# Squares of W_qkv taken during the output visits of layer 0, and a weight's low half ahead of the gate on VectorE

## The chip, the cores and the metric

The kernel runs on one core of one Trainium2 chip. The metric is device time in microseconds (us), smaller is better; a time is the median of several executions. The engines are TensorE (PE, matmuls), VectorE (DVE), ScalarE (ACT), GpSimd (POOL) and SyncE (SP), which issues the transfers (DMAs).

## The reference, cut to what matters

A trunk of two layers on x of 1024 rows and 1024 columns, in float32. Layer 0 mixes rows by a gated linear recurrence (RG-LRU), layer 1 by stick-breaking attention. Each mixer is followed by a dense SwiGLU FFN with 2816 inner columns:

```python
D_MODEL = 1024; SEQ = 1024; DEPTH = 2; D_FF = 2816

def swiglu_ffn(x, w_in, w_out):
    gu = jnp.einsum("bsd,df->bsf", x, w_in)
    h = jax.nn.silu(gu[..., :D_FF]) * gu[..., D_FF:]
    return jnp.einsum("bsf,fd->bsd", h, w_out)

for i in range(DEPTH):
    x = x + mixer[i](rms_norm(x, mix_norm[i]))
    x = x + swiglu_ffn(rms_norm(x, ffn_norm[i]), ffn_w_in[i], ffn_w_out[i])
return rms_norm(x, final_norm)
```

The attention of layer 1 begins with one projection by W_qkv (1024 x 3072). Its squares are not part of the reference: the kernel uses them for a scale, below.

## The kernel before, in words

**Number format.** Matrix products are made of float16 halves. A weight is scaled by a power of two and split into a high half, `hi = f16(scale * w)`, written by ACT (`high`, L779), and a low half, `lo = scale * w - hi`, written by DVE (`low`, L784). A product of blocks is three matmuls (`mm3`, L156 to L158): hi by hi, hi by lo of the moving side, and lo by hi; so the weight's low half is first read by the third matmul, L158. The scales come from bounds on the data, for which ACT sums squares of the weights (Square with an accumulator, L762 and L1557).

**The FFN's steps.** The function `mix_out_ffn_in` (L697, called once for each layer) holds the FFN. Its input products run in 22 steps f0 to f21, one for each block of 128 inner columns. Its output products run in 13 "visits" v0 to v12 (`VISITS`, L1245), each for some output columns and m = 2 to 4 pairs of inner blocks. Step and visit alike are a Strassen-like scheme of 7 block products in the `ORDER` 0, 1, 2, 3, 4, 6, 5 (the position in it is k), each of 3m matmuls of 128x512 (12 for m = 4). Even steps of `PAIRS` (f4, f6 to f18) and the odd ones behind them share an inner scheme for product 1. The weights of a step come as `wa`, `wb`, `wc` and `wd`; product 0 uses `wa`, product 2 `wb`, then `wc`, `wb` again, `wd` and `wc`.

**Banks.** Products 0, 2, 4 and 5 accumulate in one PSUM bank, 3 and 6 in another (`BANK`, L619). The result of the earlier product is copied out before the later one continues, so each of these products waits for a copy of the product two places ahead. In a step ACT copies most of them (`post`: L1075 after product 0, L1079 after 2, L1081, L1083, L1088), in a visit too (`post_out`: L1486, to `ta`, `tb` and `held`), and DVE adds what was copied to the residual (L1488, L1490) or adds from PSUM itself (L1492).

**The gate.** At the start of a step the gate of the block before is taken: DVE multiplies (L1093), ACT applies Silu (L1095), DVE multiplies twice more (L1097, L1099). In odd steps of `PAIRS` it comes later.

**Squares in the steps.** `weigh_out` (L1552) loads one block of 128 x 1024 weights (512 KB) by SP (L1554) into one of six norm tiles (`loose`) and, one step later, takes its squares on ACT (L1557), with the sums in a column of `wosq`. `spots` says at which step and position: in layer 1 22 blocks of ffn_w_out, in layer 0 these and 24 of W_qkv behind them, three in a step. When the last is done, DVE sums the columns (`add_up(4)`, L1294 to L1296, in v6), PE sums over partitions into `n_ps` (`next_scales`, v7) and DVE works out exponents (`next_factors`, L1341 to L1343, L1304, in v7).

**Beside it.** From f10 to f20 `split_ahead` (L1396) uses the scratch tiles `acc` and `rbc`, two halves of 128 x 512 each, and from v9 on the squares of the finished residual use them. In the visits, the moving side's blocks are brought back from memory (`bring`, by SP) and partly split there (ACT L1393, DVE L1394).

**What sets the order.** PE, ACT, DVE and POOL execute in the order in which the code is written. A dictionary `plan` maps (step, position) to small jobs and is emptied at that point by `measure`. SP's order is left to a scheduler; its queue too is served in order.

A step starts with these lines, where `odd` has been dealt with above (DVE and ACT get their instructions in this order):

```python
                elif gf is not None and s_:
                    gate(gf, 0)
                if not w.ready:
                    w.b_lo()
                    if kind == "f":
                        w.c_hi()
```

Of the kernel before, what the change touches and what calls it, by code (L numbers as in the profile page):

```python
# [8 lines left out]
F32 = mybir.dt.float32  # L9
# [4 lines left out]
AF = mybir.ActivationFunctionType  # L14
# [4 lines left out]
P = 128  # L19
S = 1024  # L20
D = 1024
ND = D // P
NT = S // P
NB = 512
NH = S // NB
DFF = 2816
NF = DFF // P
# [8 lines left out]
def trunk(  # L36
# [21 lines left out]
    nc = tc.nc  # L58
    f32 = lambda t: t.bitcast(F32)

    cp = ctx.enter_context(tc.tile_pool(name="cp", bufs=1))
# [35 lines left out]
    nc.gpsimd.memset(eps4, 0.25 * EPS)  # L97
    vc = cp.tile([P, P], F32, name="vc")

    rbc = [cp.tile([P, NB], F32, name=f"rbc{n}") for n in range(NH)]  # L100
    acc = [None] * NH
    xh, xl = [None] * ND, [None] * ND
    xstk = ExitStack()

# [167 lines left out]

    def open_acc(stk):
        pool = stk.enter_context(tc.tile_pool(name="accp", bufs=1, side="right", reuse_waits="tile"))
        acc[:] = [pool.tile([P, NB], F32, name=f"acc{n}") for n in range(NH)]

    def open_h(nm, h):
        hp = hstk.enter_context(tc.tile_pool(name=nm, bufs=1, side="right", reuse_waits="tile"))
# [19 lines left out]
    with ExitStack() as st, tc.manual_schedule(engines={E.PE, E.Activation, E.DVE, E.Pool, E.SP}):  # L298
# [45 lines left out]
        junk = sp.tile([P, D], F32, name="junk")  # L344
# [303 lines left out]
    def highest(dst, src):  # L648
        nc.vector.tensor_reduce(dst, src, axis=AX, op=ALU.max, apply_absolute_value=True)
# [47 lines left out]
    def mix_out_ffn_in(mix, bias, layer, gnext, outs):  # L697
# [8 lines left out]
        junk = sp_.tile([P, D], BF16, name="junk")  # L706
        wosq = sp_.tile([P, 64], F32, name="wosq")
        spare_ = wosq[:, 48:64]
        v, h = {}, []
        open_v(vs, v, True)  # L710
        open_acc(vs)
        open_h(f"h{layer}_", h)
        for j in range(ND // 2):
# [9 lines left out]
        if outs:  # L723
# [6 lines left out]
            class Six:  # L730
                at = 0
# [207 lines left out]
        with tc.manual_schedule(engines={E.PE, E.Activation, E.DVE, E.Pool}):  # L939
# [150 lines left out]
            def gate(f, k):  # L1090
                G, U = GT[f % 2], UT[f % 3]
                if k == 0:
                    V.tensor_mul(G, ob, G)  # L1093
                elif k == 1:
                    nc.scalar.activation(G, G, AF.Silu, scale=inv[f])  # L1095
                elif k == 2:
                    V.tensor_mul(G, ob, G)  # L1097
                else:
                    V.scalar_tensor_tensor(U, U, inv[f], G, op0=ALU.mult, op1=ALU.mult)  # L1099
# [186 lines left out]
            def add_up(what):  # L1286
                p = part16[0]
                with nc.allow_low_precision(reason="a bound alone"):
                    if what == 0:
                        V.tensor_reduce(p[:, 2:3], ymax[:, 0:8], axis=AX, op=ALU.add)  # L1290
                    elif what == 3:
                        V.tensor_reduce(p[:, 2:3], wosq[:, 0:NF], axis=AX, op=ALU.add)
                    elif what == 4:
                        V.tensor_reduce(p[:, 0:1], wosq[:, NF : NF + 3 * ND], axis=AX, op=ALU.add)  # L1294
                        V.tensor_mul(wsq[0], wsq[1][:, 0:ND], wsq[1][:, 0:ND])
                        V.tensor_reduce(p[:, 1:2], wsq[0], axis=AX, op=ALU.add)  # L1296
                    else:
                        V.tensor_reduce(tmp[:, 0:1], ymax[:, 8:16], axis=AX, op=ALU.add)
                        V.tensor_reduce(tmp[:, 1:2], wsq[0][:, 0:6], axis=AX, op=ALU.add)
                        V.tensor_add(p[:, 2:3], tmp[:, 0:1], tmp[:, 1:2])  # L1300
# [202 lines left out]
            plan = {}  # L1503
# [34 lines left out]

            plan["v", 2, 6] = [lambda: add_up(1)]
            plan["v", 3, 0] = [lambda: scales(1)]  # L1540
            spots = [(x, k) for x in range(4, 20) for k in ((0, 1, 3) if gnext else (1,) + (3,) * (x < 10))]
            rows_up = [ffn_w_out[layer][i * P : (i + 1) * P, :] for i in range(NF)]
            if gnext:
                rows_up += [w_qkv[i // 3 * P : (i // 3 + 1) * P, i % 3 * D : (i % 3 + 1) * D] for i in range(3 * ND)]
                plan["f", 4, 5] = [load_gain]
                plan["f", 5, 5] = [lambda: highest(K_M, gain_of[0])]
                plan["v", 5, 0] = [next_x]
                plan["v", 6, 5] = [lambda: add_up(4)]
                plan["v", 7, 0] = [next_scales]
                plan["v", 7, 3] = [next_factors]  # L1550

            def weigh_out(i):  # L1552
                t = loose(v)
# [8 lines left out]
            for s_, (kind, x) in enumerate(steps):  # L1562
# [12 lines left out]
                gf = x - 1 if kind == "f" else NF - 1 if x == 2 else None  # L1575
                even, odd = kind == "f" and x in PAIRS, kind == "f" and x - 1 in PAIRS
                if odd:
                    g = {1: (0,), 2: (1,), 3: (2,), 4: (3,)}
                elif gf is not None and s_:
                    gate(gf, 0)  # L1580
                if not w.ready:
                    w.b_lo()
                    if kind == "f":
                        w.c_hi()
                banks = {}
                if kind == "f":
                    rhs = rhs_in
# [285 lines left out]

    w_qkv, wq0 = attn_w_qkv[0], []
    mix_out_ffn_in(mix, V_BO, 0, V_MIX + ND, None)
    ring.close()
    NP = HEADS // 2
# [468 lines left out]

    ring.open(4)
    mix_out_ffn_in(mix[0], None, 1, None, (pos, obs, begun, psZ))

    xstk.close()  # L2350
# [40 lines left out]
```

## Time and profile before

| | |
|---|---|
| median of 3 runs | 2084.01 us |
| the runs | 2081.61, 2084.01, 2084.85 us |
| the profiled execution | 2083.18 us, its span 2081.1 us |
| granted TensorE clock, mean | 0.999 |
| instructions | 28578 |
| HBM traffic, mean over the span | 137 GB/s |

The span is the time from the first to the last instruction in the profile; the execution is some 2 us longer. Lines of the profile name a line of the kernel, an engine, an operation, the tile written and the tiles read ("out<-in"), and the shape. "Idle before" is the time an engine stood still ahead of an instruction, with the instruction that ended it behind an arrow. A window lists the busy time of each engine between two moments. In the table below the places spoken of later are put in time:

| stretch | layer 0, us | layer 1, us |
|---|---|---|
| steps f2 and f3 | 367.39 to 404.95 | 1493.29 to 1530.83 |
| steps f4 to f19 | 404.95 to 698.02 | 1530.83 to 1817.80 |
| visit v0 | 734.56 to 746.35 | |
| visit v2 | 759.96 to 778.09 | |
| visits v6 and v7 | 831.09 to 867.38 | |
| visit v9 | 885.51 to 904.80 | |

### The profile page before, as it was taken

Reading aid. Unit: us, or ns where it says so; the run is one execution under the profiler, and the core shown is the slowest. Engines: PE = TensorE matmul, PEld = TensorE weight load, DVE = VectorE, ACT = ScalarE, POOL = GpSimd, SP = SyncE. Lnnn points to the kernel's source line nnn. Section 1 sums busy time; section 2 is a strip of 40 time slices with the busy share of each in tenths; the row PEclk is TensorE's granted clock in tenths of the full one; section 3 lists DMA queues with packets and bytes.
Section 4 is the critical chain, followed back from the end, with each engine's and each line's share of the span. In section 5 each row is a group of like instructions: output and inputs, shape, how many; then the busy total and the mean of one; then the engine's idle time right before and its main releaser. Section 6 shows DMA issues by size and latency. Waiting matters only on the chain.

```text
span 2081.1 us, 28578 instructions
## 1 busy us (share of the span) xinstructions
PE 2026.6 (97%) x10059; PEld 1111.7 (53%) x10059; DVE 1847.6 (89%) x2795; ACT 1452.1 (70%) x2279; POOL 116.8 (6%) x154
## 2 busy tenths in 40 slices
PE   8999999999999999999999999999999999999998
PEld 7888885445544444444555555554445545444445
DVE  6887898989898899897999999988899899999886
ACT  6777446777878656566888888755777777665566
POOL 1000010000000000000011111212000000000002
PEclk9999999999999999999999999999999999999999
DMA  7231471675677665233887887754355546674412
GB/s 254 61 97 55 166 222 58 187 231 193 224 228 238 234 219 168 59 101 103 160 157 155 154 153 151 148 175 141 93 195 177 178 153 207 211 257 149 137 46 91
DMA packets 444000, 332.27 MB, mean 160 GB/s; under 512 B 165832, under 2 KB 361552, under 8 KB 443856
## 3 DMA queue, kind: packets, MB, share of 16 engines
q1 hardware_dynamic: 443696, 330.19, 55.0%
q8 instruction: 78, 1.28, 0.3%
q14 instruction: 66, 0.54, 0.1%
q10 hardware_dynamic: 160, 0.27, 0.0%
HBM read 215.55 MB, written 69.21 MB: 137 GB/s over the span
## 4 chain that ended last, share of the span: by engine, by line
PE 59%; DVE 21%; ACT 12%; issue 6%; DMA 2%; SPq 0%; DVEq 0%; ACTq 0%
PE p_ps L158 11%; PE p_ps L156 11%; PE p_ps L157 11%; PE a_ps L157 3%; PE a_ps L158 3%; PE a_ps L156 3%; PE ob_ps L156 2%; PE ob_ps L158 2%; PE ob_ps L157 2%; DVE wx L2152 2%; DVE wa L784 2%; DVE v L1394 2%; ACT kk L2041 1%; ACT w L2129 1%; DVE sb L799 1%
## 5 line engine op out<-in xcount | busy, mean ns | idle before, releaser
L158 PE MATMUL p_ps<-v,wb 128*128 128x512 f16 x524 | 198.8, 379 | 8.1 <-DVE wb L784 7.9
L156 PE MATMUL p_ps<-v,wb 128*128 128x512 f16 x524 | 198.5, 379 | 4.4 <-ACT G L1075 2.6
L158 PE MATMUL p_ps<-v,wc 128*128 128x512 f16 x524 | 198.6, 379 | 3.2 <-DVE wc L784 3.2
L157 PE MATMUL p_ps<-v,wc 128*128 128x512 f16 x524 | 198.6, 379 | 0.0
L157 PE MATMUL p_ps<-v,wb 128*128 128x512 f16 x524 | 198.6, 379 | 0.0
L156 PE MATMUL p_ps<-v,wc 128*128 128x512 f16 x524 | 198.5, 379 | 0.0
L158 PE MATMUL p_ps<-v,wa 128*128 128x512 f16 x396 | 150.1, 379 | 0.0
L157 PE MATMUL p_ps<-v,wa 128*128 128x512 f16 x396 | 150.1, 379 | 0.0
L156 PE MATMUL p_ps<-v,wa 128*128 128x512 f16 x396 | 150.0, 379 | 0.0
L779 ACT ACTIVATE wb<-sb,fac 128x1024 f16<-128x1024 f32 x44 | 50.5, 1148 | 108.8 <-DVE sb L799 108.8
L2151 ACT CAST wx<-w 128x512 f16<-128x512 f32 (+1 forms) x140 | 80.0, 572 | 48.4 <-DVE w L2136 26.4
L156 PE MATMUL p_ps<-v,wd 128*128 128x512 f16 x254 | 96.2, 379 | 6.6 <-ACT G L1486 3.6
L2136 DVE TENSOR_TENSOR_SCAN w<-w,unit 128x128 f32<-128x128 f32 (+1 forms) x112 | 93.4, 834 | 8.8 <-ACT w L2129 7.7
L156 PE MATMUL qk_ps<-rh,w 128*128 128x512 f16 x264 | 101.0, 383 | 0.0
L157 PE MATMUL qk_ps<-rh,w 128*128 128x512 f16 x264 | 100.0, 379 | 0.3 <-DVE rh L250 0.3
L158 PE MATMUL qk_ps<-rh,w 128*128 128x512 f16 x264 | 100.0, 379 | 0.0
L2129 ACT ACTIVATE w<-z_ps,rs 128x512 f32<-128x512 f32 (+2 forms) x168 | 96.4, 577 | 4.6 <-PE z_ps L2092 3.0
L158 PE MATMUL p_ps<-v,wd 128*128 128x512 f16 x254 | 96.3, 379 | 1.5 <-DVE wd L784 1.5
L156 PE MATMUL a_ps<-xh,whi 128*128 128x512 f32 x248 | 97.0, 391 | 0.0
L2091 PE MATMUL z_ps<-kk,q 128*128 128x256 f32 (+1 forms) x192 | 94.1, 490 | 2.9 <-ACT w L2129 1.4
L157 PE MATMUL a_ps<-xl,whi 128*128 128x512 f32 x248 | 96.6, 390 | 0.1
L158 PE MATMUL a_ps<-xh,wlo 128*128 128x512 f32 x248 | 96.6, 389 | 0.0
(489 smaller groups left out, 5591.1 us busy)
## 6 DMA issues: line engine op xcount, KB each, us to landing
raw<-in_ffn_w_in SPq DMA_DIRECT2D x80, 512.0 KB, 4.3
pd<-U SPq DMA_DIRECT2D x90, 256.0 KB, 2.4
loose<-in_ffn_w_out SPq DMA_DIRECT2D x44, 512.0 KB, 4.2
raw<-pd SPq DMA_DIRECT2D x66, 256.0 KB, 3.7
row<-pd SPq DMA_DIRECT2D x62, 256.0 KB, 3.9
raw<-in_ffn_w_out SPq DMA_DIRECT2D x56, 256.0 KB, 3.3
loose<-in_attn_w_qkv SPq DMA_DIRECT2D x24, 512.0 KB, 3.8
raw<-in_attn_w_qkv SPq DMA_DIRECT2D x24, 512.0 KB, 4.6
```

The source lines that it names most:

```text
L156: nc.tensor.matmul(ps, lhsT=wh, rhs=mh, start=first, stop=False, **kw)
L157: nc.tensor.matmul(ps, lhsT=wh, rhs=ml, start=False, stop=False, **kw)
L158: nc.tensor.matmul(ps, lhsT=wl, rhs=mh, start=False, stop=last, **kw)
L779: nc.scalar.activation(h, r, AF.Copy, scale=up)
L784: V.scalar_tensor_tensor(l, r, up, h, op0=ALU.mult, op1=ALU.subtract)
L799: V.tensor_sub(self.part(self.sb, 0), self.part(self.rb, 0), self.part(self.ra, 0))
L1394: V.scalar_tensor_tensor(lo, raw, power_of(p), hi, op0=ALU.mult, op1=ALU.subtract)
L2091: nc.tensor.matmul(ps[:, 0 : c1 - c0], lhsT=lhsT, rhs=KK[q][hx][:, 0, c0:c1], start=True, stop=False)
L2129: nc.scalar.activation(F, ps[:, 0:n], AF.Sigmoid, scale=rs[:, j : j + 1])
L2136: nc.vector.tensor_tensor_scan(rev, rev, unit[:, NB - n :][:, ::-1], 0.0, op0=ALU.mult, op1=ALU.add)
L2151: nc.scalar.copy(wx[:, 0:m, 0], F)
L2152: nc.vector.tensor_sub(wx[:, 0:m, 1], F, wx[:, 0:m, 0])
```

## The change

Three things change.

1. `rbc` and `acc` become one tile of 128 x 1024 each, whose halves are slices.
2. In layer 0 the 24 squares of W_qkv leave the steps. `spots` now has layer 1's pattern in both layers: 22 squares at position 1 of f4 to f19 and position 3 of f4 to f9. The W_qkv squares go to visits v0, v1, v2, v5, v6 and v7 (two, two, six, three, six, five). Their blocks are no longer loaded into norm tiles but in turn into `acc` and `rbc`: the first two loads are issued in f21, and the load of square i+2 right behind square i, from which it frees its tile. The three jobs that follow the last square move by about one visit: `add_up(4)` from v6 to v7, `next_scales` and `next_factors` from v7 to v8.
3. In both layers, where a step starts with a gate, DVE first writes the low half of `wb` and then the gate's first product; it was the other way round.

```diff
-    rbc = [cp.tile([P, NB], F32, name=f"rbc{n}") for n in range(NH)]
-    acc = [None] * NH
+    rbc2 = cp.tile([P, S], F32, name="rbc")
+    rbc = [rbc2[:, n * NB : (n + 1) * NB] for n in range(NH)]
+    acc, acc2 = [None] * NH, [None]
...
-        acc[:] = [pool.tile([P, NB], F32, name=f"acc{n}") for n in range(NH)]
+        acc2[0] = pool.tile([P, S], F32, name="acc")
+        acc[:] = [acc2[0][:, n * NB : (n + 1) * NB] for n in range(NH)]
...
-            spots = [(x, k) for x in range(4, 20) for k in ((0, 1, 3) if gnext else (1,) + (3,) * (x < 10))]
+            spots = [(x, k) for x in range(4, 20) for k in (1,) + (3,) * (x < 10)]
             rows_up = [ffn_w_out[layer][i * P : (i + 1) * P, :] for i in range(NF)]
             if gnext:
-                rows_up += [w_qkv[i // 3 * P : (i // 3 + 1) * P, i % 3 * D : (i % 3 + 1) * D] for i in range(3 * ND)]
+                visits = {0: (2, 5), 1: (1, 4), 2: range(6), 5: (1, 3, 5), 6: range(6), 7: range(5)}
+                places = [("v", x, k) for x, ks in visits.items() for k in ks]
+
+                def load_qkv(i):
+                    dst = (acc2[0], rbc2)[i % 2]
+                    nc.sync.dma_start(dst, w_qkv[i // 3 * P : (i // 3 + 1) * P, i % 3 * D : (i % 3 + 1) * D])
+
+                def weigh_qkv(i):
+                    t = (acc2[0], rbc2)[i % 2]
+                    nc.scalar.activation(junk, t, AF.Square, accum_out=wosq[:, NF + i : NF + i + 1])
+                    if i + 2 < 3 * ND:
+                        load_qkv(i + 2)
+
+                for i, at in enumerate(places):
+                    plan[at] = [lambda i=i: weigh_qkv(i)]
+                for i in range(2):
+                    plan.setdefault(("f", NF - 1, 4 + i), []).append(lambda i=i: load_qkv(i))
...
-                plan["v", 6, 5] = [lambda: add_up(4)]
-                plan["v", 7, 0] = [next_scales]
-                plan["v", 7, 3] = [next_factors]
+                plan["v", 7, 6] = [lambda: add_up(4)]
+                plan["v", 8, 1] = [next_scales]
+                plan["v", 8, 4] = [next_factors]
...
-                elif gf is not None and s_:
-                    gate(gf, 0)
                 if not w.ready:
                     w.b_lo()
                     if kind == "f":
                         w.c_hi()
+                if gf is not None and s_ and not odd:
+                    gate(gf, 0)
```

The lines of the changed kernel stand two further down from the third hunk on: L1095 is the gate, L786 the low half, L1488 the copies of a visit; the squares of ffn_w_out stay with `weigh_out`, those of W_qkv are L1555 and their loads L1551.

VectorE at the start of step f6 in layer 0, before the change. `G` is the gate's tile, `ob` the PSUM tile that it multiplies, `known` a maximum over a loaded row of gains, which only layer 0 takes here:

```order
L802 TENSOR_TENSOR s_3661<-sb,raw 128x512
L649 TENSOR_REDUCE known<-loose 128x1
L1109 TENSOR_TENSOR ta<-U_2698 128x512
L1093 TENSOR_TENSOR G_2696<-ob,G_2696 128x1024
L784 SCALAR_TENSOR_TENSOR wb<-sb,fac_99,wb 128x1024
L784 SCALAR_TENSOR_TENSOR wc<-raw,fac_99,wc 128x1024
```

And after it:

```order
L804 TENSOR_TENSOR s_3651<-sb,raw 128x512
L651 TENSOR_REDUCE known<-loose 128x1
L1111 TENSOR_TENSOR ta<-U_2696 128x512
L786 SCALAR_TENSOR_TENSOR wb<-sb,fac_98,wb 128x1024
L1095 TENSOR_TENSOR G_2694<-ob,G_2694 128x1024
L786 SCALAR_TENSOR_TENSOR wc<-raw,fac_98,wc 128x1024
```

The gate and the low half of `wb` have changed places; the low half of `wc` stays third.

ScalarE in visit v6 of layer 0, from the copy of product 0 on, before the change. `ta`, `tb` and `held` are where products are copied to, `v_` rows split blocks of the moving side, and `wa` to `wd` rows write high halves of weights:

```order
L1486 ACTIVATE ta<-p_ps,rx 128x512
L779 ACTIVATE wc<-raw,gx 128x1024
L1393 ACTIVATE v_3_2649<-raw_3_7143,gx 128x512
L1393 ACTIVATE v_2_2644<-raw_2_7166,gx 128x512
L1393 ACTIVATE v_3_2645<-raw_3_7183,gx 128x512
L1486 ACTIVATE tb<-p_ps,rx 128x512
L779 ACTIVATE wd<-s_7117,gx 128x512
L779 ACTIVATE wa<-raw,gx 128x1024
L1486 ACTIVATE held<-p_ps,rx 128x512 x2
```

And after it:

```order
L1488 ACTIVATE ta<-p_ps,rx 128x512
L781 ACTIVATE wc<-raw,gx 128x1024
L1555 ACTIVATE junk,wosq<-rbc 128x1024
L1395 ACTIVATE v_3_2647<-raw_3_7095,gx 128x512
L1395 ACTIVATE v_2_2642<-raw_2_7120,gx 128x512
L1555 ACTIVATE junk,wosq<-acc 128x1024
L1395 ACTIVATE v_3_2643<-raw_3_7137,gx 128x512
L1488 ACTIVATE tb<-p_ps,rx 128x512
L781 ACTIVATE wd<-s_7067,gx 128x512
L781 ACTIVATE wa<-raw,gx 128x1024
L1555 ACTIVATE junk,wosq<-rbc 128x1024
L1488 ACTIVATE held<-p_ps,rx 128x512
```

Between two copies there now stands one square or two, each of which reads a tile that a load has to fill first.

## The prediction

> **What bounds the kernel now.** I read the page first, then the table of windows over the FFN steps, then the engines' timelines at the steps that came out long. The engine row (engine, busy us, share of the span, instructions) and two matmul groups (busy, mean ns | idle before, who ended most of it):
>
> ```profile
> PE 2026.6 (97%) x10059; PEld 1111.7 (53%) x10059; DVE 1847.6 (89%) x2795; ACT 1452.1 (70%) x2279; POOL 116.8 (6%) x154
> ...
> L158 PE MATMUL p_ps<-v,wb 128*128 128x512 f16 x524 | 198.8, 379 | 8.1 <-DVE wb L784 7.9
> L156 PE MATMUL p_ps<-v,wb 128*128 128x512 f16 x524 | 198.5, 379 | 4.4 <-ACT G L1075 2.6
> ```
>
> PE is the bound. The change removes no matmul, so all it can win is PE's waits, and of those the ones at product 2's weights `wb`: their low half (DVE, L784) and the copy that frees product 2's bank (ACT, L1075). Where they lie shows in windows. Each row is from and to, us, then busy us of PE, PEld, DVE, ACT, POOL, then clock, DMA share and GB/s. A window holds an even step of PAIRS and the odd one behind it. Layer 1: f4+5, f12+13 and f18+19; the windows between are like the nearer end (four of 35.69 to 35.71, four of 36.04 to 36.05).
>
> ```profile
> 1530.83:1566.52 35.69, 35.69 (x189) 18.21 (x188) 31.71 (x51) 26.65 (x41) 0.00 (x0) 1.00 0.57 184
> 1673.61:1709.66 36.05, 35.86 (x188) 18.15 (x187) 33.40 (x53) 26.10 (x41) 0.00 (x0) 1.00 0.51 169
> 1781.75:1817.80 36.05, 35.87 (x189) 18.09 (x188) 33.17 (x51) 25.07 (x38) 0.00 (x0) 1.00 0.68 230
> ```
>
> The same eight windows of layer 0, f4+5 to f18+19:
>
> ```profile
> 404.95:440.64 35.69, 35.69 (x189) 18.22 (x188) 31.90 (x51) 28.50 (x45) 0.00 (x0) 1.00 0.66 214
> 440.64:477.37 36.73, 35.86 (x189) 18.14 (x187) 33.23 (x53) 29.17 (x47) 0.00 (x0) 1.00 0.67 222
> 477.37:513.08 35.71, 35.71 (x189) 18.23 (x188) 32.72 (x57) 28.84 (x47) 0.19 (x1) 1.00 0.63 199
> 513.08:549.34 36.26, 35.85 (x189) 18.24 (x187) 32.77 (x53) 29.26 (x49) 0.00 (x0) 1.00 0.71 225
> 549.34:586.21 36.87, 36.17 (x188) 18.09 (x187) 33.51 (x53) 29.91 (x49) 0.00 (x0) 1.00 0.68 221
> 586.21:623.08 36.87, 36.17 (x188) 18.13 (x187) 33.51 (x53) 29.91 (x49) 0.00 (x0) 1.00 0.74 236
> 623.08:661.18 38.10, 36.18 (x189) 18.09 (x188) 33.60 (x53) 30.04 (x49) 0.00 (x0) 1.00 0.72 235
> 661.18:698.02 36.84, 36.16 (x188) 18.15 (x187) 33.59 (x51) 27.12 (x42) 0.00 (x0) 1.00 0.77 257
> ```
>
> An unhindered pair takes 35.69. Over that, layer 0 loses 1.04 + 0.02 + 0.57 + 1.18 + 1.18 + 2.41 + 1.15 = 7.55 us, layer 1 4 x 0.36 = 1.44. Steps f2+f3, layer 0 and layer 1:
>
> ```profile
> 367.39:404.95 37.56, 36.66 (x172) 16.30 (x171) 35.41 (x54) 26.01 (x43) 0.00 (x0) 1.00 0.63 194
> 1493.29:1530.83 37.54, 36.66 (x172) 16.34 (x171) 35.41 (x54) 25.99 (x43) 0.00 (x0) 1.00 0.64 195
> ```
>
> Two unhindered steps of this kind take 2 x 18.16 = 36.32 (window v7, below), so 1.24 + 1.22 = 2.46 more goes here. In all 11.45 us of waits lie in steps that the change touches.
>
> **The change, part by part.** *Low half ahead of the gate, both layers.* DVE and PE at f6 of layer 0 (start, us, instruction):
>
> ```profile
> 441.81 1.21 DVE L649 TENSOR_REDUCE known<-loose 128x1 f32<-128x1024 f32 x1
> ...
> 443.53 1.22 DVE L1093 TENSOR_TENSOR G<-ob,G 128x1024 f32<-128x1024 f32 x1
> 444.67 1.27 DVE L784 SCALAR_TENSOR_TENSOR wb<-sb,fac,wb 128x1024 f16<-128x1024 f32 x1
> ```
> ```profile
> 446.00 0.39 PE L158 MATMUL p_ps<-v,wb 128*128 128x512 f16 x1 [0.87 <-DVE wb L784]
> ```
>
> The first matmul that reads the low half waits 0.87 and starts at 446.00, when that half (444.67 + 1.27 = 445.94) is done. With the two changed over, it is done at 443.53 + 1.27 = 444.80, 1.14 sooner, against a window 1.04 too long: the wait goes, by 0.1. At f12 of layer 1 the wait is a third of that:
>
> ```profile
> 1675.83 1.22 DVE L1093 TENSOR_TENSOR G<-ob,G 128x1024 f32<-128x1024 f32 x1
> 1676.96 1.27 DVE L784 SCALAR_TENSOR_TENSOR wb<-sb,fac,wb 128x1024 f16<-128x1024 f32 x1
> ```
> ```profile
> 1677.18 1.15 ACT L1095 ACTIVATE G<-G,fac 128x1024 f32<-128x1024 f32 x1
> ...
> 1680.72 0.59 ACT L1079 COPY G<-p_ps 128x512 f32<-128x512 f32 x1
> ```
> ```profile
> 1684.36 0.38 PE L156 MATMUL p_ps<-v,wb 128*128 128x512 f16 x1
> ```
>
> The price is a later gate. It would end at 1675.83 + 1.27 + 1.22 = 1678.3, so ACT's Silu (L1095) starts 1.1 later, and behind Silu on ACT stand the inner weights, a square and the copy L1079, which would end at 1682.4. PE needs its bank at 1684.36: 2 us of cover, so I cost the later gate at nothing. Without that cover it would be up to 1.1 at each of 26 gates. The low half of `wc`, third in both orders, doesn't move. So the swap takes f2+f3 (2.46), f12 to f18 of layer 1 (1.44), and in layer 0 f6 (1.04) and the same 0.36 at f12 to f18 (1.44): 6.38.
>
> *Squares out of layer 0's steps.* With them layer 0 does 24 squares more than layer 1 in the same steps, and its windows are longer by more than the swap explains: 0.57 + 0.82 + 0.82 + 2.05 + 0.79 = 5.05. Here ACT is late with the copy L1075. Layer 1, which has already the pattern that layer 0 gets, shows none of it, so I take 5.05. Bounds: nothing, if something else of layer 0 delays that copy, and 5.05. Sum of the gains: 6.38 + 5.05 = 11.43.
>
> *Squares into the visits.* Windows v0, v2, v6, v7 and v9 of layer 0; one square (L1557, two instructions); the landing time of their loads (min, median, max), and the page's median for them alone:
>
> ```profile
> 734.56:746.35 11.79, 9.89 (x44) 3.89 (x43) 11.79 (x20) 8.79 (x15) 0.00 (x0) 1.00 0.93 307
> 759.96:778.09 18.13, 18.13 (x86) 8.23 (x85) 17.43 (x23) 9.72 (x12) 0.00 (x0) 1.00 0.33 110
> 831.09:849.22 18.13, 18.13 (x85) 8.23 (x84) 16.18 (x23) 9.98 (x13) 0.00 (x0) 1.00 0.20 59
> 849.22:867.38 18.16, 18.16 (x87) 8.22 (x86) 13.50 (x28) 7.91 (x12) 3.10 (x7) 1.00 0.20 59
> 885.51:904.80 19.29, 18.28 (x85) 8.22 (x84) 19.14 (x29) 14.66 (x23) 0.00 (x0) 1.00 0.22 69
> ```
> ```profile
> L1557 ACT ACTIVATE junk<-loose x68: 1042/1052/1067, 408.2 to 1803.8; 128x1024 bf16<-128x1024 f32 x68
> L1557 ACT ACTIVATION_READ_ACCUMULATOR junk<-loose x68: 186/191/202, 409.2 to 1804.8; 128x1 f32 x68
> ...
> DMA to landing us min/median/max: 3.4/4.2/6.9
> ```
> ```profile
> loose<-in_attn_w_qkv SPq DMA_DIRECT2D x24, 512.0 KB, 3.8
> ```
>
> A square is 1.05 + 0.19 = 1.24 us of ACT. Six in v2 make 9.72 + 7.44 = 17.2 of 18.13, six in v6 17.4, five in v7 14.1, two in v0 11.3 of 11.79. ACT holds them, but only if each starts on time, and here is the new wait: the load of square i+2 is issued (SP) when square i has freed its half of the ring, so a square comes every (T + 1.24) / 2 us, T being issue to landing. A product takes 18.13 / 7 = 2.59. With T = 3.8 the ring turns every 2.52, in time; with 4.2 every 2.72, which is 0.13 late for each of 17 squares, 2.2 in all. I take the middle of the two, 1.1, since the row's 4.2 has ffn_w_out's loads in it. What is queued behind a waiting square is the copy of a product's bank, and PE needs that bank one product later:
>
> ```profile
> 844.30 0.69 ACT L1486 ACTIVATE held<-p_ps,rx 128x512 f32<-128x512 f32 x1 [1.90 <-PE p_ps L158]
> ```
>
> This copy waited 1.90 for PE, so ACT has time to spare there now, which a square takes. The Trainium skill, page "DMA: Bandwidth & Descriptors", section "Rules for kernel authors", says to issue a transfer early and wait for it late, and its section "Latency and other measured facts" gives HBM access 0.2 us on average and 2 us at high load. By those figures a load in a loaded stretch would take an estimated 4.2 + 1.8 = 6.0, a square would be 1.03 late and 17 of them would cost 17.5 instead of 1.1; DMA shares of 0.20 to 0.33 in v2, v6 and v7 speak against high load, and no trace here shows these loads in the visits.
>
> The other seven squares (v0 two, v1 two, v5 three) stand alone, with a load that had several products to land. Bounds: nothing, or all seven in full, 8.7, if each stood before a copy that PE awaits. v0 is tight (DVE 11.79 of 11.79, PE already waiting 1.9), where a square may lie behind what PE waits for; I take 0.5 in all.
>
> The loads themselves change queue places as well. SP issues in order, and a load that waits for its square holds what stands behind it: the output weights (L1265 after the change) and the products brought in (L1419), both for a visit to come. They have some 18 us, a visit, and lose at most one turn of the ring, 2.7, so I cost that at nothing; if a visit's weights had no such lead, it would be up to 2.7 in each of v2, v6 and v7. The loads of the products start earlier in f19 to f21, since the norm tiles come free sooner, and later in v1 and v2, for the same reason without cost.
>
> *Small operations moved to v7 and v8.* DVE in v7 of layer 0:
>
> ```profile
> 849.42 0.17 DVE L1294 TENSOR_REDUCE part<-wosq 128x1 bf16<-128x24 f32 x1
> ...
> 849.77 0.74 DVE L1492 SCALAR_TENSOR_TENSOR g<-p_ps,rx,g 128x512 f32<-128x512 f32 x1
> ...
> 862.13 0.16 DVE L1341 TENSOR_SCALAR wosq<-wosq 128x3 f32<-128x3 f32 x1
> ...
> 862.93 0.74 DVE L1394 SCALAR_TENSOR_TENSOR v<-row,gx,v 128x512 f16<-128x512 f32 x1
> ```
>
> They take 0.35 and 0.80. In v7 DVE has 18.16 - 13.50 = 4.7 idle and they cost nothing. One step later DVE stays filled to the end of v9 (19.14 of 19.29, and PE waits there, 19.29 against 18.16), so they count one for one: 1.15. Bounds: nothing, and 1.15.
>
> *rbc and acc as one tile each.* The halves are the same bytes, so nothing.
>
> Sum: 11.43 - 1.1 - 0.5 - 1.15 = 8.7 us off. The profiled execution took 2083.18 (span 2081.1), 0.83 under the median of 2084.01; it becomes 2074.5, and the median **2075.3**.
>
> **The rivals.** *The ring is too slow (slower).* The place is v2, v6 and v7. Against the other terms' 9.8 us of gain, 17 squares that are each 0.58 late break even, which is T = 5.1, and beyond T = 5.6 the kernel is measurably slower. With the 6.9 of the row's maximum a square is 1.48 late, 25.2 in all: 2084.0 - 9.8 + 25.2 = 2099.4. For it: ACT is 95% full in v2 and v6, so it catches nothing up, and each load has its own wait for ACT ahead of it. Against: the medians 3.8 and 4.2 come from windows with DMA shares of 0.7, twice those of v2. Chance 0.08. The page's rule on early issue, above, gives this outcome too.
>
> *The swap buys nothing.* The wait passes on to `wc` or the gate, since DVE is 33.4 of 36.05 busy. Then only 5.05 - 2.75 = 2.3 is won: 2081.7. Against it: `wc` is needed a product after `wb` and doesn't move. Chance 0.08.
>
> *Late copies pass to the tail.* A copy behind a square reaches DVE late, and the blocks of v8 and v9, where DVE has no room, start late. I price it at 2.2 for the ring and 0.6, half a square, for each of the seven: 2.2 + 4.2 + 1.15 = 7.6, gain 3.9, so 2080.1. For it: v9's 19.14 of 19.29. Against: PE's one product of slack. Chance 0.13.
>
> *It doesn't do what it says.* Layer 0's copies are late for other reasons, such as stores that hold their targets, and the squares' removal wins nothing: 6.38 - 2.75 = 3.6, 2080.4, or worse with the ring. Chance 0.03.
>
> **How the numbers follow.** The forecast has 0.68. About 0.2%, 4.2 us, is what a measurement here can tell from no change, so the bounds are 2079.8 and 2088.2. Faster: 0.68, and of the cases around 2080 to 2082, whose terms can fall either way by some us, 0.02 + 0.08, together 0.78. Same: 0.06 + 0.05 + 0.02 = 0.13. Slower: the ring's 0.08 and 0.01 of the last, 0.09. The range: all costs nil gives 2072.6, less 1.1, a third of the 3.2 us between the three times before, 2071.5; upward it takes in the late copies, the undone gain and the lost swap, to 2081.7. Only the slow ring and some of the outer edges are left out.
>
> **What would show it.** Right: pairs of layer 0 at 35.7 to 35.8 each, f2+f3 at 36.3 to 36.5 in both layers, no wait of PE's at `wb`'s low half in them; v2, v6 and v7 at 18.1 to 18.8; v8+v9 1 us longer. The ring shows in the squares' idle time "<-DMA acc" and "<-DMA rbc", and in landing times above 4. Wrong: v2, v6 or v7 above 20, or pairs that stay at 36 and more.

## The result, and the profile after

The changed kernel takes 2076.38 us (median of 8 runs, 2074.87 to 2078.46), the kernel before 2082.62 in the same comparison (8 runs, 2081.22 to 2084.85). The ratio is 0.9971, 95% interval 0.996 to 0.9982: 6.2 us less, where 8.7 were forecast. The profiled execution of the changed kernel took 2078.07, its span 2076.0, 5.1 less than before; it is one of the slower of the eight.

The page's engine row and the same two matmul groups, which now have line numbers one higher:

```profile
PE 2025.5 (98%) x10059; PEld 1113.1 (54%) x10059; DVE 1846.9 (89%) x2795; ACT 1451.3 (70%) x2279; POOL 119.6 (6%) x154
...
L159 PE MATMUL p_ps<-v,wb 128*128 128x512 f16 x524 | 198.7, 379 | 3.9 <-DVE wb L786 3.6
...
L157 PE MATMUL p_ps<-v,wb 128*128 128x512 f16 x524 | 198.5, 379 | 2.9 <-ACT ta L1488 0.8
```

The engines do the same work. PE's idle time ahead of `wb`'s low half has more than halved (8.1 to 3.9). Ahead of the product's first matmul it fell from 4.4 to 2.9; of that, the copy of product 0 in the steps made 2.6 before (L1075) and makes 0.6 now (L1077). Where it was won and where not, in windows: layer 0's f2+3, f4+5, f6+7 and f12+13, then layer 1's f2+3, f4+5 and f12+13.

```profile
367.32:404.18 36.86, 36.65 (x172) 16.40 (x171) 34.31 (x52) 25.82 (x42) 0.00 (x0) 1.00 0.64 198
404.18:440.28 36.10, 35.98 (x189) 18.21 (x187) 32.89 (x53) 26.61 (x41) 0.00 (x0) 1.00 0.55 183
440.28:476.76 36.48, 35.85 (x189) 18.23 (x187) 33.30 (x53) 26.76 (x43) 0.00 (x0) 1.00 0.61 195
548.16:583.85 35.69, 35.69 (x188) 18.23 (x187) 33.41 (x53) 25.88 (x41) 0.00 (x0) 1.00 0.53 170
1489.39:1526.24 36.85, 36.65 (x172) 16.39 (x171) 34.31 (x52) 25.89 (x42) 0.00 (x0) 1.00 0.66 197
1526.24:1562.34 36.10, 35.98 (x188) 18.23 (x187) 32.89 (x53) 26.61 (x41) 0.00 (x0) 1.00 0.55 182
1669.44:1705.12 35.68, 35.68 (x188) 18.21 (x187) 33.40 (x53) 25.86 (x41) 0.00 (x0) 1.00 0.53 171
```

From f8 on every pair of both layers is at 35.7, as forecast. But f2+3 got 0.7 shorter and not 1.24, f4+5 got 0.41 longer, and f6+7 is 36.48 and not 35.7. The first half of f6+7 is as forecast; the second half has a new wait. VectorE at the end of f6, ScalarE and PE in f7 (times start f7 at 458.44):

```profile
457.79 0.69 DVE L801 TENSOR_TENSOR sb<-raw 128x512 f32<-128x512 f32 x1
```
```profile
458.52 1.15 ACT L781 ACTIVATE wb<-sb,fac 128x1024 f16<-128x1024 f32 x1 [2.23 <-DVE sb L801]
...
463.17 0.57 ACT L1077 COPY G<-p_ps 128x512 f32<-128x512 f32 x1
```
```profile
463.79 0.38 PE L157 MATMUL p_ps<-v,wb 128*128 128x512 f16 x1 [0.63 <-ACT G L1077]
```

VectorE forms `sb` late, ScalarE waits for it before it can write `wb`'s high half, and everything behind that on ScalarE is late, the copy that frees PE's bank too. The 2.23 us are not the sign in themselves: at f13 ScalarE waits 2.42 us at the same place and PE loses nothing. But at f13 it starts on `wb` 0.84 us before the step does, at f7 0.08 us after. PE lost its wait at f6, so it meets the next late instruction at f7.

In layer 0 the visits pay. Windows v0, v3, v6 and v9 (v1 is 0.06 longer, the rest as before):

```profile
727.38:739.28 11.90, 9.72 (x44) 3.96 (x43) 11.90 (x20) 9.83 (x17) 0.00 (x0) 1.00 0.95 303
771.08:789.84 18.76, 18.32 (x87) 8.25 (x85) 15.91 (x32) 11.60 (x19) 2.51 (x11) 1.00 0.63 201
824.69:843.94 19.25, 18.46 (x85) 8.14 (x84) 15.17 (x21) 15.17 (x24) 0.00 (x0) 1.00 0.65 193
880.23:900.40 20.17, 18.46 (x85) 8.14 (x84) 20.03 (x33) 14.88 (x23) 1.64 (x4) 1.00 0.21 67
```

v0 costs 0.11, v3 0.61, v6 1.12 and v9 0.88, with v1 2.78 in all; 2.75 were forecast. The waits of the squares for their loads (idle time, times; then issue to landing), and in v6 ScalarE and PE:

```profile
  DMA acc<-in_attn_w_qkv: 4.8, 5
  DMA rbc<-in_attn_w_qkv: 1.3, 2
...
DMA to landing us min/median/max: 3.5/4.2/5.8
```
```profile
833.10 1.06 ACT L1555 ACTIVATE junk<-acc 128x1024 bf16<-128x1024 f32 x1 [1.14 <-DMA acc<-in_attn_w_qkv]
...
838.05 0.67 ACT L1488 ACTIVATE held<-p_ps,rx 128x512 f32<-128x512 f32 x1
```
```profile
838.77 0.38 PE L157 MATMUL p_ps<-v,wd 128*128 128x512 f16 x1 [0.47 <-ACT held L1488]
```

A square waits 1.14 us for its load, the copy `held` comes late behind it, and PE waits. ScalarE stood still 6.1 us for the ring, of which PE felt a part.

### The profile page after: what moved, and what is told of

Its sections match the earlier page's. It is cut to its first block, busy times and chain, and to the rows that moved or that the text cites. A ratio compares the mean times of both kernels' runs of the same rounds, so it can differ in the third digit from the quotient of the medians.

```text
span 2076.0 us, 28549 instructions
## 1 busy us (share of the span) xinstructions
PE 2025.5 (98%) x10059; PEld 1113.1 (54%) x10059; DVE 1846.9 (89%) x2795; ACT 1451.3 (70%) x2279; POOL 119.6 (6%) x154
## 4 chain that ended last, share of the span: by engine, by line
PE 63%; DVE 18%; ACT 10%; issue 6%; DMA 2%; SPq 0%; DVEq 0%; ACTq 0%
PE p_ps L157 12%; PE p_ps L159 12%; PE p_ps L158 12%; PE a_ps L158 3%; PE a_ps L159 3%; PE a_ps L157 3%; PE ob_ps L157 2%; PE ob_ps L158 2%; PE ob_ps L159 2%; DVE wx L2170 2%; DVE v L1396 2%; ACT kk L2059 1%; DVE wa L786 1%; ACT w L2147 1%; DVE w L2154 1%
```

## The experiments

Each window below has the columns as before. Times of steps come from the windows; two kernels agree in them within some 0.03 us where nothing differs, so one profiled execution is enough for those. The exceptions are listed in the last section.

**swap_alone.** The low half ahead of the gate, in the kernel before:

```diff
-                elif gf is not None and s_:
-                    gate(gf, 0)
                 if not w.ready:
                     w.b_lo()
                     if kind == "f":
                         w.c_hi()
+                if gf is not None and s_ and not odd:
+                    gate(gf, 0)
```

> Only the low half of wb ahead of the gate, in both layers; the W_qkv squares stay in the steps. Theory A (the prediction's term): the swap alone takes 6.4 us off, 1.24 at f2+f3 of each layer, 1.04 at f6 of layer 0, 0.36 at each of f12 to f18 in both. Theory B (the trace after the change): the waits taken away at f2, f3 and f6 come back in part one or two steps later, 0.4 at f4+f5 of each layer and 0.8 at f7 of layer 0, because VectorE and ScalarE are then the later ones; 3.9 us off. Rival: with a square ahead of it the Silu in layer 0 hides the later gate, so nothing comes back there, and it is 5 or more.

Measured: 2080.29 us against 2082.65, ratio 0.9989 (0.998 to 0.9998), 2.4 off, less than either theory. Layer 1's steps and f2 to f7 of layer 0 are as in the changed kernel. But in layer 0, where the squares still stand, f12+13 is not shorter:

```profile
546.88:583.81 36.93, 36.00 (x188) 18.19 (x187) 33.51 (x53) 29.98 (x49) 0.00 (x0) 1.00 0.69 221
```

36.93 where it was 36.87: the even step is 0.54 shorter, the odd one 0.59 longer. With late copies the wait goes from one step to the next. The rival falls too, since f4+5 of layer 0 is 36.10 here as well.

**squares_alone.** All of the change but the swap:

```diff
+                elif gf is not None and s_:
+                    gate(gf, 0)
                 if not w.ready:
                     w.b_lo()
                     if kind == "f":
                         w.c_hi()
-                if gf is not None and s_ and not odd:
-                    gate(gf, 0)
```

> Only the squares moved (with the tiles and the three late jobs); the gate stays ahead of the low half. Theory (both the prediction and the trace after): 5.05 us off in f10 to f19 of layer 0, 2.8 back in the visits, so 2.3 us off. If the two parts need each other it is another number: the pairs f12 to f18 of layer 0 would then not come down to layer 1's 36.05.

Measured: 2080.2 us, ratio 0.999 (0.9981 to 0.9999), 2.45 off. Its f12+13:

```profile
547.64:583.69 36.05, 35.87 (x189) 18.16 (x188) 33.40 (x53) 26.12 (x41) 0.00 (x0) 1.00 0.51 168
```

That is layer 1's number of before, and it is so in f10 to f19 throughout: with 24 squares gone the windows f10+11 to f18+19 sum to 5.07 less, as forecast. But not all of it is shown to be the squares'. 1.2 of it lies at f17, which took 19.25 in the kernel before, where f13 and f15 took 18.03. There the copy L1075 waited for something else, a store of `G` to memory that still held the copy's target:

```profile
647.57 0.58 ACT L1075 COPY G<-p_ps 128x512 f32<-128x512 f32 x1 [1.10 <-DMA pd<-G]
```

The same wait makes f17 of layer 1 0.7 longer in the run changed_again and 1.1 in nine_back, with no square of W_qkv in that layer. In layer 0 it is there in all three kernels that keep such squares in the steps, and in few of the others; whether the squares' loads lengthen it, no run separates. For the squares on ScalarE 3.85 is shown.

The two parts alone give 2.4 each and together 6.2. The medians can't tell the 1.4 between, but the windows show it: it is 0.36 at each of f12, f14, f16 and f18 of layer 0, which the swap wins only where the squares are gone.

**no_reload and no_squares.** In the first, the squares read what the first two loads brought, and 22 loads are left out. In the second there are no W_qkv squares and no loads; the sums are set to 1.

```diff
-                    if i + 2 < 3 * ND:
-                        load_qkv(i + 2)
```
```diff
-                for i, at in enumerate(places):
-                    plan[at] = [lambda i=i: weigh_qkv(i)]
-                for i in range(2):
-                    plan.setdefault(("f", NF - 1, 4 + i), []).append(lambda i=i: load_qkv(i))
+                plan["v", 0, 2] = [lambda: nc.gpsimd.memset(wosq[:, NF : NF + 3 * ND], 1.0)]
```

> The changed kernel without the loads of squares 2 to 23: each square reads what the first two loads brought. It leaves out 22 loads, so its scale for W_qkv comes from two blocks. If the turn of the two tiles (a square waiting for its load) is what the visits pay for, v6 loses its 1.1 and v3 its 0.6, and the kernel is 1.5 to 2 us faster than the changed one, 8 off against before. If it is the squares' own time on ScalarE, it stays within 0.5 us of the changed kernel, 6 to 6.5 off.

> The changed kernel without the 24 W_qkv squares and their loads (the sums are set to 1): the floor for the visits. The three late jobs stay in v7 and v8. Expected: v0, v3 and v6 as before the change, so 1.9 us faster than the changed kernel, 8 off against before. v9 shows the price of the small operations alone: 0.9 us over before if they are the cause there, nothing if it was late copies passed on.

Measured: 2076.28 (ratio 0.997, 0.9959 to 0.9982) and 2074.62 (0.9963, 0.9951 to 0.9976). v6 and v9 of the first, then of the second:

```profile
825.65:844.28 18.63, 18.30 (x86) 8.15 (x85) 16.28 (x23) 15.79 (x25) 0.00 (x0) 1.00 0.20 57
880.56:900.59 20.03, 18.47 (x86) 8.14 (x85) 19.88 (x31) 14.72 (x23) 1.51 (x4) 1.00 0.21 68
```
```profile
824.29:842.42 18.13, 18.13 (x85) 8.19 (x84) 16.18 (x23) 9.98 (x13) 0.00 (x0) 1.00 0.20 59
878.71:898.79 20.08, 18.46 (x85) 8.14 (x84) 19.93 (x32) 14.77 (x23) 1.57 (x4) 1.00 0.21 67
```

Without the loads v6 loses 0.62 of its 1.12 and v3 nothing. In other executions with the same squares v6 took 19.06 to 19.25, so the ring costs 0.4 to 0.6, all of it in v6. That v9 differs by 0.15 lies within what v9 shows between two executions of one kernel (20.02 and 20.17). The 0.50 that v6 keeps is a wait of PE's for `wb`'s low half. Without squares v0, v3 and v6 are as before the change, and v9 keeps 0.79: there it is the small operations, not late copies. The median of no_reload doesn't show its 0.6; that is below what a median of these runs tells.

**gate_first_f2f3 and gate_first_f4.** The gate goes first again at f2 and f3, or at f4, in the changed kernel:

```diff
+                first = kind == "f" and x in (2, 3)
+                if first:
+                    gate(gf, 0)
                 if not w.ready:
...
-                if gf is not None and s_ and not odd:
+                if gf is not None and s_ and not odd and not first:
                     gate(gf, 0)
```

The second has `x == 4` in the first line.

> The changed kernel with the gate ahead of the low half again at f2 and f3 alone, both layers. Theory B (a wait taken away at f2 and f3 comes back at f4 and f5, because VectorE is behind by then): f2 and f3 are back at 18.93 and 18.62, and f4 and f5 lose their new 0.13 and 0.28 (18.16 and 17.53). Rival (the swap at f4 itself delays something there): f4 and f5 stay at 18.29 and 17.81.

> The changed kernel with the gate ahead again at f4 alone, both layers. Theory B: f4 and f5 keep 0.4 of waits or get more. Rival (the swap at f4 is what delays the copies): both come down to 18.16 and 17.53, and the kernel is 0.8 us faster than the changed one.

Measured, one execution each: 2078.18 and 2077.51. Windows f2+3 and f4+5 of the first, f4+5 of the second:

```profile
366.80:404.34 37.54, 36.65 (x171) 16.34 (x170) 35.40 (x54) 26.00 (x43) 0.00 (x0) 1.00 0.64 193
404.34:440.03 35.69, 35.69 (x188) 18.22 (x187) 31.80 (x51) 26.54 (x41) 0.00 (x0) 1.00 0.56 185
```
```profile
404.04:440.40 36.36, 36.00 (x189) 18.14 (x188) 32.81 (x53) 26.84 (x41) 0.00 (x0) 1.00 0.55 181
```

With the gate first at f2 and f3 their wait is back, and f4+5 has none. With the gate first at f4 that pair gets 0.26 worse, not better. So Theory B holds: 0.41 of the 0.70 won at f2+3 comes back two steps later. VectorE's work of f2 to f5 has not become less: it is busy 35.40 and 31.80 us in the two windows with the gate first, and 34.31 and 32.89 in the changed kernel, 67.2 both times; 1.1 us of it have moved on into f4+5.

**reduce_later.** The maximum over the gains one step later:

```diff
-                plan["f", 4, 5] = [load_gain]
-                plan["f", 5, 5] = [lambda: highest(K_M, gain_of[0])]
+                plan["f", 5, 5] = [load_gain]
+                plan["f", 6, 5] = [lambda: highest(K_M, gain_of[0])]
```

> The changed kernel with the maximum over the gains of layer 0's next norm (1.13 us of VectorE at the start of f6), and its load, one step later, at the start of the odd step f7. Theory: VectorE is 1.13 us late through f6 because of it, so the high half of f7's wb and the copy behind it are late; with it moved f7 falls from 18.32 to 17.53, f6 stays at 18.16, 0.8 us in all. Rival: f7 takes the same delay in another place and keeps 0.5 or more, or f8 gets it.

Measured, one execution: 2076.64. The window f6+7:

```profile
440.65:476.34 35.69, 35.69 (x188) 18.21 (x187) 33.30 (x53) 26.75 (x43) 0.00 (x0) 1.00 0.63 199
```

36.48 is now 35.69, and f8+9 is unchanged. The same operation, one step later, costs nothing: in f7 VectorE stands idle 1.2 us before `wc` and takes it there.

**spread.** The squares at other places, and the small operations in v7:

```diff
-                visits = {0: (2, 5), 1: (1, 4), 2: range(6), 5: (1, 3, 5), 6: range(6), 7: range(5)}
+                visits = {0: (2, 5), 1: (1, 4), 2: (1, 3, 5), 3: range(6), 5: (1, 3, 5), 6: range(6), 7: (0, 1)}
...
-                plan["v", 7, 6] = [lambda: add_up(4)]
-                plan["v", 8, 1] = [next_scales]
-                plan["v", 8, 4] = [next_factors]
+                plan.setdefault(("v", 7, 2), []).append(lambda: add_up(4))
+                plan.setdefault(("v", 7, 3), []).append(next_scales)
+                plan.setdefault(("v", 7, 6), []).append(next_factors)
```

> The changed kernel with the W_qkv squares spread otherwise: two in v0, two in v1, three in v2, six in v3, three in v5, six in v6, two in v7, and the three jobs behind them in v7 (positions 2, 3 and 6) instead of v7 to v8. Theory: the price of v9 (0.8) is the small operations in a stretch where VectorE has no idle time, and that of v3 (0.6) six squares in v2 that make the sums at its end late; both go, v6 keeps 1.1 or less, and v3 may get up to 1.1 of its own: 0.3 to 1.4 us faster than the changed kernel, 6.5 to 7.5 off. Rival: v9 keeps its 0.8 because of late copies, then it is the same as the changed kernel.

Measured: 2077.92, ratio 0.9976 (0.9967 to 0.9985), not faster than the changed kernel. Windows v3, v4 and v9:

```profile
769.07:788.20 19.13, 18.40 (x86) 8.23 (x85) 13.87 (x28) 14.93 (x26) 3.05 (x11) 1.00 0.81 248
788.20:805.44 17.24, 14.25 (x64) 6.05 (x63) 16.85 (x29) 14.73 (x26) 0.00 (x0) 1.00 0.95 302
...
880.62:899.91 19.29, 18.30 (x86) 8.22 (x85) 19.14 (x29) 14.67 (x23) 0.00 (x0) 1.00 0.22 70
```

v9 is back at 19.29, as it was before the change, so its price was the small operations. But six squares in v3 make v4 1.43 longer (15.81 in the changed kernel, with VectorE filled to the last), v5 0.73 and v3 0.37. The price of a square thus seems to depend on what follows: in v2 and v6, behind which VectorE has idle time, six cost 0.6 and 1.1.

**changed_again, two_moves and three_moves.** The changed kernel again, and two attempts to better it. In both, the maximum is moved as in reduce_later and the scale of v2's sums by one product. In three_moves the squares also end sooner:

```diff
-            plan["v", 3, 0] = [lambda: scales(1)]
+            plan["v", 3, int(gnext is not None)] = [lambda: scales(1)]
```
```diff
-                visits = {0: (2, 5), 1: (1, 4), 2: range(6), 5: (1, 3, 5), 6: range(6), 7: range(5)}
+                visits = {0: (2, 5), 1: (1, 4), 2: range(6), 5: (1, 3, 4, 5), 6: range(7), 7: (0, 1, 2)}
...
-                plan["v", 7, 6] = [lambda: add_up(4)]
-                plan["v", 8, 1] = [next_scales]
-                plan["v", 8, 4] = [next_factors]
+                plan.setdefault(("v", 7, 3), []).append(lambda: add_up(4))
+                plan.setdefault(("v", 7, 4), []).append(next_scales)
+                plan.setdefault(("v", 7, 6), []).append(next_factors)
```

> The changed kernel itself, on the same chip as the next two: 6 us off against before, as measured.

> The changed kernel with two single steps moved in layer 0: the maximum over the gains to f7 (as in reduce_later), and the scale from the sums at v2's end (PE's n_ps) from v3's first product to its second. Theory: f7's 0.8 and v3's 0.6 are each the delay of that one instruction, so both go, 1.4 us faster than the changed kernel, 7.5 off. Rival for v3: ScalarE's six squares in v2 have put VectorE behind in general, and v3 keeps its 0.6 at another wait.

> As two_moves, and the squares end four positions sooner (v5 has four, v6 seven, v7 three), so that the three jobs behind them run in v7 (positions 3, 4 and 6). Theory: v9 loses 0.8 to 0.9, as the small operations run where VectorE has idle time; v6 gains 0.2 to 0.6 with its seventh square: 0.3 to 0.7 us faster than two_moves, 8 off. Rival: a square more in v5, where VectorE is 18.73 of 19.04 busy, costs what v9 gives.

Measured: 2076.34 (ratio 0.9967, 0.9954 to 0.9979), 2076.52 (0.9962, 0.9949 to 0.9976) and 2079.83 (0.9986, 0.9977 to 0.9995). Of two_moves the windows v3 and v7, and ScalarE in v7:

```profile
771.36:789.51 18.15, 18.15 (x86) 8.25 (x85) 15.89 (x32) 11.68 (x19) 3.50 (x11) 1.00 0.67 209
...
843.51:862.27 18.76, 18.29 (x85) 8.22 (x84) 11.88 (x16) 14.35 (x23) 0.00 (x0) 1.00 0.66 196
```
```profile
857.30 1.06 ACT L1555 ACTIVATE junk<-acc 128x1024 bf16<-128x1024 f32 x1 [1.11 <-DMA acc<-in_attn_w_qkv]
...
858.97 0.67 ACT L1488 ACTIVATE held<-p_ps,rx 128x512 f32<-128x512 f32 x1
```

Both waits are gone (f7 0.79, v3 0.61), so each was the delay of that one instruction. But 0.63 is back in v7 (18.13 in the changed kernel), where a copy stands behind a square that waits for its load. A likely reason is that PE comes to v7 sooner while the ring doesn't turn faster (loads land in 4.3 us there, in 4.2 in the changed kernel); with one execution this is not shown. So 0.8 of the 1.4 is left, and the medians can't tell it. In three_moves, PE in v7 waits for the sums:

```profile
862.18 0.16 PE L264 MATMUL n_ps<-part,one 128*128 128x2 bf16 x1 [4.11 <-DVE part L1298]
```

Ten squares in ten products in a row are more than the ring delivers: ScalarE waited 8.8 us for the loads, 6.1 in the changed kernel. The last square came some 5 us late, the sums one product ahead of their use gave no cover, and v7 took 24.12. v9 was at 19.28. This is the mechanism of the prediction's first rival: with the squares a little denser and no room behind them, the ring decides, and more than half of the gain is lost.

**nine_back.** As two_moves, with nine squares in the steps again and room between the fifteen others:

```diff
+            NS = 9 if gnext else 0
+            spots += [(10 + y, 3) for y in range(NS)]
...
-                visits = {0: (2, 5), 1: (1, 4), 2: range(6), 5: (1, 3, 5), 6: range(6), 7: range(5)}
+                visits = {0: (2, 5), 1: (1, 4), 2: (0, 2, 4, 5), 5: (1, 3, 5), 6: (0, 2, 3, 4)}
...
-                plan["v", 7, 6] = [lambda: add_up(4)]
-                plan["v", 8, 1] = [next_scales]
-                plan["v", 8, 4] = [next_factors]
+                plan.setdefault(("v", 7, 0), []).append(lambda: add_up(4))
+                plan.setdefault(("v", 7, 2), []).append(next_scales)
+                plan.setdefault(("v", 7, 5), []).append(next_factors)
```

> As two_moves, with nine of the 24 squares back in the steps (position 3 of f10 to f18, through the norm tiles) and fifteen in the visits: two in v0, two in v1, four in v2, three in v5, four in v6, none in v7; the three jobs behind them in v7 (positions 0, 2 and 5). Theory: one square more in a step costs nothing once positions 0 and 1 are not loaded too (f8+9 of layer 0 carries that now at 35.71); the ring of two tiles keeps up when not every product has a square, so v6 and v7 lose 1.1 and 0.6, and the small operations leave v8 and v9, which lose 0.9: about 3 us faster than the changed kernel, 9 off against before. Rival: ScalarE in f10 to f18 is late with any second square, 0.3 to 0.6 in each odd step, 3 to 5 in all, and the gain is eaten.

Measured: 2080.14, ratio 0.999 (0.9981 to 0.9999). The visits do what was expected (v7 18.16, v9 19.29), but the rival is right, and by more: f11 to f19 are 6.2 us longer, 0.7 of it at f17 by the store's wait. Windows f12+13 and v6:

```profile
545.88:582.81 36.93, 36.00 (x188) 18.19 (x187) 33.51 (x53) 27.84 (x45) 0.00 (x0) 1.00 0.62 192
...
827.59:846.22 18.63, 18.30 (x85) 8.11 (x84) 16.33 (x23) 15.12 (x23) 0.00 (x0) 1.00 0.46 142
```

One square of W_qkv in a step, two squares with that of ffn_w_out, brings f12+13 to the 36.93 of swap_alone, which has three. How it does that shows at the end of f12: ScalarE, VectorE and PE in nine_back (f13 starts at 564.19), then VectorE in the changed kernel (there f13 starts at 566.32):

```profile
558.87 1.05 ACT L1578 ACTIVATE junk<-loose 128x1024 bf16<-128x1024 f32 x1
...
559.91 0.71 ACT L1395 ACTIVATE rbc<-acc,gx 128x512 f16<-128x512 f32 x1
...
564.57 1.15 ACT L781 ACTIVATE wb<-sb,fac 128x1024 f16<-128x1024 f32 x1 [2.43 <-DVE sb L801]
...
569.22 0.57 ACT L1077 COPY G<-p_ps 128x512 f32<-128x512 f32 x1
```
```profile
560.66 0.75 DVE L1396 SCALAR_TENSOR_TENSOR rbc<-acc,gx,rbc 128x512 f16<-128x512 f32 x1 [1.24 <-ACT rbc L1395]
```
```profile
569.84 0.38 PE L157 MATMUL p_ps<-v,wb 128*128 128x512 f16 x1 [0.93 <-ACT G L1077]
```
```profile
561.57 0.75 DVE L1396 SCALAR_TENSOR_TENSOR rbc<-acc,gx,rbc 128x512 f16<-128x512 f32 x1 [0.21 <-ACT rbc L1395]
```

The square stands ahead of `split_ahead`'s high half (L1395), for which VectorE waits 1.24 us with its whole queue. That delay goes by way of `sb` and `wb`'s high half, which starts 0.38 us after f13 does (in the changed kernel 0.84 before), to the next step's copy, and PE waits there. In the kernel before, VectorE waits the same 1.24 us for the split at f12. Steps f4 to f9, which have a square at the same position, have no `split_ahead`. So it isn't ScalarE's load that made these steps slow (28 of 37 us; f8+9 of the kernel before had 28.8 of 35.7 and lost nothing), but a square ahead of an instruction that a filled VectorE awaits.

## Why the prediction was right, and where it wasn't

The forecast time, 2075.3, is 1.1 from the measured one, but that is in part luck: it was taken from a time before of 2084.01, which is 2082.62 over more runs. The gain was forecast 2.5 too large. Of the signs that were to show it right, f8 to f19 and v8+v9 came as stated; f2+3 (36.9), f4+5 (36.1), f6+7 of layer 0 (36.5) and v6 (19.25) did not.

*Squares out of the steps, 5.05.* Right in kind, and 5.07 by the windows, but that size is in part luck. The term counts 2.05 for f16+17, and 1.2 of that was the wait for a store of `G`, which the prediction had among its rivals ("stores that hold their targets") and not in this term. 3.85 are shown to be the squares' on ScalarE. The cause stated, ScalarE late with L1075, is the end of the chain; nine_back shows its beginning, the split behind the square.

*Swap, 6.38.* The mechanism was right, the size was not. What was won at each place: f12 to f18 1.44 in each layer, as forecast; f2+3 0.70 and 0.69 instead of 1.24 and 1.22, less 0.41 given back at f4+5 in each layer; f6+7 0.25 instead of 1.04; f20 0.08 in each layer. That is 1.44 + 1.44 + 0.29 + 0.28 + 0.25 + 0.16 = 3.9, and the runs say the same: the changed kernel against squares_alone is 2076.4 against 2080.2. The step that failed is in the sentence "So the swap takes f2+f3 (2.46) ... f6 (1.04)". It took each wait as gone, and did not ask what is late next on an engine with little idle time. The rival that the wait passes on came true by a half: 0.41 of 0.70 at f2+3, 0.79 of 1.04 at f6. In f6 the forecast's 0.1 of margin was right for that step, but the 1.13 us that stood ahead of the low half still stood ahead of everything behind it (reduce_later removes it and f7 is whole). The later Silu, costed at nothing, did cost nothing where it was priced, at f12 of layer 1, which is whole.

*The ring, 1.1.* It cost 0.4 to 0.6 (no_reload), in v6 alone; v2 and v7 lost nothing. T was 4.2, as in the row, with DMA shares of 0.65 to 0.82 in v2, v6 and v7, where the rows of before had 0.20 to 0.33. By the Trainium skill, page "DMA: Bandwidth & Descriptors", section "Latency and other measured facts", an estimated 6.0 was to be feared at high load; no landing took more than 5.8 in this execution, and the median didn't move (4.0 to 4.5 in the other runs with this ring, with single loads of up to 6.9). The advice of the section "Rules for kernel authors" fits three_moves, where PE waited 4.1 us in the end because squares waited for loads that could not be issued earlier.

*Other squares, 0.5.* The seven in v0, v1 and v5 cost 0.17: 0.11 in v0, 0.06 in v1, nothing in v5. But the six in v2 and the six in v6 cost 1.1 beyond the ring, for which the prediction had no term: 0.61 in v3 and the 0.50 in v6 that is left without loads. Squares in v2 delay VectorE's sums at its end, for which PE has a matmul (n_ps) at the start of v3; two_moves takes that matmul one product later, and the 0.61 is gone.

*Small operations, 1.15.* They cost 0.8, in v9, where the forecast had them (no_squares keeps the price, spread moves them and loses it).

The costs together, 2.78, hit the forecast's 2.75 by luck: the ring and the small operations were sized too large and the squares' own time too small. The whole is then 3.9 + 5.07 - 2.78 = 6.2, which is the difference of the medians; their interval, 3.7 to 8.3, would allow much else. Of the rivals, the slow ring was not reached by this kernel but by three_moves, and "late copies pass to the tail" did not happen (no_squares).

What stays open: how much of f17's 1.2 comes with the squares' loads, and whether a kernel with two_moves' edits and the sums further ahead of their use beats the changed one measurably. No run shows either.

## What to carry to other kernels

When a wait is taken from an engine that is the bound, ask which instruction is late next at the same places. Here half of a wait and more came back one or two steps later, at f4+5 and f7. The share of busy time doesn't say where: f12 to f18 kept all of their gain with VectorE 33.4 of 35.7 us busy, f4+5 lost with 32.9 of 36.1. A filler instruction is priced by what stands behind it in its own queue and by who awaits that, not by its duration or its engine's load: the same 1.24 us square cost nothing in f8 and f9, some 0.05 in v0 and some 0.6 in f12 and f13. With a ring of two buffers, a load has only the time of one consumer's turn to land unseen; leave a gap between its consumers, or room before the one who needs the last.

## What the runs showed of the hardware

A wait of PE cost more than its length. In three_moves PE stood still for 4.2 us in v7, and then the clock was granted at half; the windows from the wait on:

```profile
858.00:862.18 4.18, 0.07 (x2) 0.00 (x1) 2.34 (x7) 4.13 (x7) 0.00 (x0) 1.00 0.01 2
862.18:864.00 1.82, 1.82 (x8) 0.75 (x8) 1.82 (x3) 0.00 (x0) 0.00 (x0) 0.83 0.03 9
864.00:865.00 1.00, 1.00 (x4) 0.42 (x3) 1.00 (x2) 0.00 (x0) 0.00 (x0) 0.50 0.00 0
865.00:866.00 1.00, 1.00 (x4) 0.32 (x3) 0.97 (x4) 0.06 (x1) 0.00 (x0) 0.50 0.00 0
866.00:867.00 1.00, 1.00 (x4) 0.39 (x3) 1.00 (x2) 1.00 (x2) 0.82 (x2) 0.60 0.00 0
867.00:869.00 2.00, 2.00 (x11) 0.89 (x10) 1.55 (x3) 0.70 (x2) 0.22 (x1) 1.00 0.00 0
```

The column behind POOL's is the clock: 0.50 from about 863.4 to 866.8, which made the visit some 1.7 us longer beside the 4.3 of the wait (24.12 against 18.13). The first microsecond of matmuls after the wait still ran at full clock. The Trainium skill, page "TensorE: Matmul & The Clock Gate", section "Part 1: The HAM clock gate (the "warmup" mystery)", has the clock at half after an idle stretch of about 3.4 us, and at full again after as long a busy one. The half clock here lasted 3.4 us, which fits. But a much shorter wait was enough elsewhere: in swap_alone PE waited 2.0 us for the copy in f17 of layer 0, and the clock was at half from 646.1 to 649.5, again 3.4 us. With the 1.7 us that this cost, f17 took 21.34. In four of the fourteen profiled executions, that of the changed kernel among them, it was also at half for 3.4 us between 1338 and 1346 in the attention, where no single wait was longer than 1.9. A wait of 1.6 us in v4 of layer 0 left the clock at full in all fourteen. So the length of one wait doesn't decide, and here the measurement goes before the page's idle stretch; what does decide, these runs don't show.

Two more things bear on how to read such small differences. The windows of FFN steps repeat from one execution to the next within 0.03 us, with few exceptions (f17 was up to 1.1 longer in some, f3 of layer 1 0.3 to 0.4 in two, v7 0.3 in one; v6 and v9 vary by 0.2). The attention part between the layers varied from 517.9 to 518.9 us with nothing changed in it, and the moment at which f2 of layer 0 starts from 365.3 to 369.7. A change of 0.6 us is thus read from a step's window, f17 apart, and not from the medians.
